# First-layer expert blocks in runs of six, with one product cut in two at each run's head, and another division of the routing among three engines

## The chip, the cores and the metric

The kernel runs on one core of a Trainium2 chip. The time is the device time of one execution in microseconds (us). A core has a matrix engine (TensorE, PE in the rows; its weight loads are listed apart as PEld), three engines for element-wise work (VectorE or DVE, ScalarE or ACT, GpSimd or POOL), and queues of DMA transfers, which SyncE (SP) issues here. Each engine works through its own instructions in order and waits for the others by semaphores.

## What is computed

A decoder layer over 256 tokens of width 1024, in 32-bit floats. The last part takes more than two thirds of the time: a layer of 16384 single-neuron experts, of which every token uses 128 (8 heads, 16 each).

```python
def token_chunk(xc):
    q = (xc @ w_q).reshape(PEER_TOK_CHUNK, PEER_HEADS, 2, half)
    s = jnp.einsum("thpd,hpnd->thpn", q, subkeys)
    s1, i1 = lax.top_k(s[:, :, 0], PEER_TOPK)
    s2, i2 = lax.top_k(s[:, :, 1], PEER_TOPK)
    cand_s = (s1[..., :, None] + s2[..., None, :])
    cand_i = (i1[..., :, None] * PEER_NKEYS + i2[..., None, :])
    top_s, top_pos = lax.top_k(cand_s, PEER_TOPK)
    e = jnp.take_along_axis(cand_i, top_pos, axis=-1)
    g = jax.nn.softmax(top_s, axis=-1)
    a = jax.nn.gelu(jnp.einsum("td,thkd->thk", xc, w_down[e]))
    return jnp.einsum("thk,thkd->td", g * a, w_up[e])
```

Ahead of it stand an attention block, a gating block and a cross-attention, and behind it a normalisation.

## The kernel before

The kernel does not gather experts. It computes all 16384 neurons for all 256 tokens and multiplies by a matrix G that holds the softmax weight of each chosen expert and zero elsewhere.

**First layer.** `down` computes one block of 128 experts: 24 products of 128x128 weights with 256 columns (the tokens), summed in one buffer (tile A, two buffers). Every float is split into a part `hi` that TensorE's format holds and a rest `lw`; for each of the 8 slices of the width come three products, hi weights with `mgh` (hi of the tokens), hi weights with `mgl` (their rest), and lw weights with `mgh`. ScalarE then applies the gelu and frees the buffer (tile aring). There are 128 such blocks, d0 to d127.

**Second layer.** One block takes the gelu of 128 experts times G (tile ga, split into gahl) as stationary operand and adds 12 products of 512 columns to the result (tile y). There are 128 such blocks, called u.

**Weights.** SyncE loads 512 KB for each block (tile raw, four buffers). `conv_to` makes `hi` on ScalarE and then `lw` on the engine that `lo_engine` names, two blocks ahead of use (`LEAD`), three buffers each.

**Order.** `plan` writes the order of d, g and u steps: 27 d blocks; then 16 g steps with 22 d blocks between them (a g step builds a piece of G for the first 64 experts of each group); then 64 u blocks with 42 d blocks spread evenly among them, one at a time; then 16 more g steps with 22 d blocks; then 64 u blocks with the last 15 d blocks spread among them. In the g stretches d blocks stand alone, and six times as a pair, in each of the two.

**Routing.** The first 26 d blocks are the work that TensorE has while the other engines choose the experts. `best` (VectorE) finds the 16 best scores M and places X of each head's halves. XF is X as floats, the first half times 128. `candidates` adds pairs: CS from the scores (VectorE) and CE from the places (GpSimd). Pieces of work on VectorE then choose 16 of the 50 candidates of each head and token (max, match_replace, max_index) and look their places up (L850, L840), until R holds places and weights. A list of estimated lengths decides between which pieces a `down` is written, and with it its `lw`, so VectorE works through the pieces and the `lw` of the d blocks in that order.

Of the kernel before, what the change touches and what calls it, by code (L numbers as in the profile page):

```python
# [21 lines left out]
AF = mybir.ActivationFunctionType  # L22
OP = mybir.AluOpType
# [4 lines left out]
S = 256  # L28
KD = 8
# [3 lines left out]
QI = 64  # L33
# [7 lines left out]
D0, D1 = 22, 4  # L41
# [2 lines left out]
NC = sum(NCAND)  # L44

N_XO, N_PQ = 4, 16
FIRST = 5


def plan():  # L50
    steps = []
    nd = 0

    def d():
        nonlocal nd
        if nd < 128:
            steps.append(("d", nd))
            nd += 1

    def g(q):  # L60

        first, room = nd, RING + q * QI - nd
        for s in range(S // TG):
            steps.append(("g", q, s))
            while nd < first + (s + 1) * room * TG // S:
                d()

    for _ in range(D0 + D1 + 1):
        d()
    g(0)  # L70
    done, want_end = 0, D0 + D1 + 1 + QI - nd
    for n in range(QI):
        steps.append(("u", n))
        want = (n + 1) * want_end // QI
        while done < want:
            d()
            done += 1
    g(1)
    left = 128 - nd
    done = 0  # L80
    for n in range(QI):
        steps.append(("u", QI + n))
        want = min(left, (n + 1) * left // (QI - 8))
        while done < want:
            d()
            done += 1
    return steps


def body(tc, I, out, dbg=None):  # L90
# [3 lines left out]
    V, A, P, T, SY = nc.vector, nc.scalar, nc.gpsimd, nc.tensor, nc.sync  # L94
# [26 lines left out]
    def lo_engine(m):  # L121
        kind, idx = stream[m]
        if kind == "f":
            return V if idx < nf - N_PQ + 4 else P
        if kind == "d" and idx < FIRST:
            return P
        return V

# [34 lines left out]
    def sl(k):  # L163
        return (slice(None), k, slice(None))
# [12 lines left out]
    def mm3(ps, w, wsl, x, xsl, start, stop):  # L177
        (wh, wl), (xh, xl) = w, x
        T.matmul(ps, wh[wsl], xh[xsl], start=start, stop=False)  # L179
        T.matmul(ps, wh[wsl], xl[xsl], start=False, stop=False)  # L180
        T.matmul(ps, wl[wsl], xh[xsl], start=False, stop=stop)  # L181
# [197 lines left out]
    for c in range(4):  # L379
        for nm in ("q", "k"):  # L380
            first = c == 0
            ps = tblock(take("f"), xg, mid=(sqp.matmul if nm == "q" else rope_norm) if first else None)
# [139 lines left out]
    for c in range(4):  # L522
        ps = tblock(take("f"), xg)
# [270 lines left out]
    def mblock():  # L794
        return pp.tile([128, 512], F32, name="m", bufs=2)

    def down(i2):
        w = take("d")
        ps = pp.tile([128, S], F32, name="A", bufs=2)
        for k in range(KD):  # L800
            mm3(ps, w, (slice(None), slice(k * 128, k * 128 + 128)), h3, sl(k), k == 0, k == KD - 1)
        a = gp.tile([128, S], F32, name="aring", bufs=RING)
        A.activation(a, ps, AF.Gelu_apprx_tanh)  # L803
        Aq[i2] = a
# [3 lines left out]


    XF = rp.tile([128, 8, 2, 2, 16], F32, name="XF", bufs=1)  # L810
    V.tensor_copy(XF, X1)
    V.tensor_scalar(XF[:, :, :, 0], XF[:, :, :, 0], 128.0, None, op0=OP.mult)
    CS = rp.tile([128, 8, 2, NC], F32, name="CS", bufs=1)
    CE = rp.tile([128, 8, 2, NC], F32, name="CE", bufs=1)

# [46 lines left out]
    def piece(us, fn, *args):  # L862
        work.append((us, lambda: fn(*args)))

    piece(2.7, candidates, CS, M1, V)
    for (h, t) in ht:
        piece(0.12, V.max, M2[:, h, t, 0:8], CS[:, h, t])
    for (h, t) in ht:
        piece(0.18, V.match_replace, rep2[:, h, t], M2[:, h, t, 0:8], CS[:, h, t], LOW)
# [4 lines left out]
    for (h, t) in ht:  # L874
        piece(0.18, V.max_index, X2[:, h, t, 8:16], M2[:, h, t, 8:16], rep2[:, h, t])
    piece(0.4, V.tensor_copy, XP, X2.rearrange("p h t k -> p (h t) k"))
    piece(0.0, P.tensor_sub, gw, M2, M2[:, :, :, 0:1].to_broadcast([128, 8, 2, 16]))
    for (p, c) in ranks:
        piece(0.15 + 2 * 16 * (17 - p) / 960, lookup, p, c)
    piece(0.3, fold)  # L880
    n, spent = 0, 0.0
    for (us, fn) in work:
        fn()
        spent += us
        while n < D0 and spent > 1.55 * (n + 1) - 2.5:
            down(n)
            n += 1
            if n == FIRST - 2:
                candidates(CE, XF, P)
    while n < D0:  # L890
        down(n)
        n += 1
# [142 lines left out]
    for n, x in enumerate(rest):  # L1035
        if x[0] == "u" and x[1] >= 128 - TAILN:
            break
        if x[0] != "g":
            for nxt in rest[n + 1:n + 3]:
                if nxt[0] == "u" and nxt[1] // QI in Gq:  # L1040
                    up_a(nxt[1])
                    later.append(lambda i2=nxt[1]: up_b(i2))
        if x[0] == "d":
            down(x[1])
            if x[1] == 127:
                A.activation(warm, ones, AF.Sqrt)
        elif x[0] == "g":
            if ng_ < len(gsteps) and gsteps[ng_][1] == x[1]:
                gprep(gsteps[ng_][1], gsteps[ng_][2])
                ng_ += 1  # L1050
            gstep(x[1], x[2])
        else:
            up_a(x[1])
            up_b(x[1])
            w = take("u")
            for t in range(2):
                umm(w, UP[x[1]], t)
            del UP[x[1]]
            if x[1] == QI - 12:
                gprep_a(1, 0)  # L1060
            if x[1] == QI - 9:
                gprep_b(1, 0)
            if x[1] == QI - 6:
                gprep_c(1, 0)
                ng_ += 1
# [118 lines left out]
```

## Time and profile before

| | |
|---|---|
| median of 3 runs | 1043.78 us (1043.71 to 1044.43) |
| the profiled execution, its own time | 1042.34 us |
| its span, first to last instruction | 1040.6 us |
| TensorE busy | 1026.7 us, 99% of the span |
| VectorE, ScalarE, GpSimd busy | 73%, 57%, 6% |
| chain that ended last | 89% TensorE, 8% VectorE |

The profile has the start and duration of every instruction, and what an engine waited for. Products overlap on TensorE, and their listed ends are modelled, so the pace of products is read from the number that starts in a stretch, not from their durations.

### The profile page before, as it was taken

Reading aid. Unit: us, or ns where it says so; the run is one execution under the profiler, and the core shown is the slowest. Engines: PE = TensorE matmul, PEld = TensorE weight load, DVE = VectorE, ACT = ScalarE, POOL = GpSimd, SP = SyncE. Lnnn points to the kernel's source line nnn. Section 1 sums busy time; section 2 is a strip of 40 time slices with the busy share of each in tenths; the row PEclk is TensorE's granted clock in tenths of the full one; section 3 lists DMA queues with packets and bytes.
Section 4 is the critical chain, followed back from the end, with each engine's and each line's share of the span. In section 5 each row is a group of like instructions: output and inputs, shape, how many; then the busy total and the mean of one; then the engine's idle time right before and its main releaser. Section 6 shows DMA issues by size and latency. Waiting matters only on the chain.

```text
span 1040.6 us, 19734 instructions
## 1 busy us (share of the span) xinstructions
PE 1026.7 (99%) x7862; PEld 951.5 (91%) x7862; DVE 760.2 (73%) x1505; ACT 594.4 (57%) x936; POOL 58.1 (6%) x51
## 2 busy tenths in 40 slices
PE   8999999999999899999999999999999999999997
PEld 7989999999999899998889889889999988888886
DVE  6765787789999899865556555565799666666666
ACT  6865745576644477754444544445677645454454
POOL 0400000006730000000000000000000000000000
PEclk9999999999999999999999999999999999999999
DMA  8743655555456434555555565555543555555552
GB/s 283 241 134 130 204 165 176 167 185 162 164 174 202 152 123 149 157 184 191 192 191 193 187 198 185 191 193 184 164 154 130 187 196 188 197 188 198 187 198 103
DMA packets 52076, 185.84 MB, mean 179 GB/s; under 512 B 5904, under 2 KB 6544, under 8 KB 51856
## 3 DMA queue, kind: packets, MB, share of 16 engines
q1 hardware_dynamic: 51264, 183.20, 53.8%
q8 instruction: 61, 1.00, 0.4%
q0 software_dynamic: 288, 1.05, 0.3%
q10 hardware_dynamic: 432, 0.34, 0.1%
q14 instruction: 31, 0.25, 0.1%
HBM read 183.52 MB, written 1.05 MB: 177 GB/s over the span
## 4 chain that ended last, share of the span: by engine, by line
PE 89%; DVE 8%; ACT 1%; DMA 1%; issue 1%; DVEq 0%; ACTq 0%
PE y L1016 11%; PE y L1019 11%; PE y L1015 11%; PE A L179 10%; PE A L181 9%; PE A L180 9%; PE mm L179 6%; PE mm L180 6%; PE mm L181 6%; DVE lw L142 3%; PE m L988 2%; PE m L987 2%; DVE jk L850 1%; DMA raw<-in_wf 1%; DVE acc L840 1%; PE nat L313 1%
## 5 line engine op out<-in xcount | busy, mean ns | idle before, releaser
L142 DVE TENSOR_TENSOR lw<-raw,hi 128x1024 fp32r<-128x1024 f32 (+1 forms) x310 | 378.8, 1223 | 229.4 <-ACT hi L140 228.8
L140 ACT CAST hi<-raw 128x1024 fp32r<-128x1024 f32 (+1 forms) x341 | 355.3, 1043 | 189.4 <-issue 142.9
L181 PE MATMUL A<-mgh,lw 128*128 128x256 f32 x1024 | 287.5, 281 | 3.1 <-DVE lw L142 3.1
L179 PE MATMUL A<-mgh,hi 128*128 128x256 f32 x1024 | 290.1, 283 | 0.0
L180 PE MATMUL A<-mgl,hi 128*128 128x256 f32 x1024 | 287.2, 281 | 0.0
L181 PEld LDWEIGHTS A<-mgh,lw 128*128 128x128 f32 x1024 | 195.9, 191 | 3.5 <-DVE lw L142 3.5
L1015 PE MATMUL y<-hi,gahl 128*128 128x512 f32 x504 | 196.1, 389 | 0.0
L1016 PE MATMUL y<-lw,gahl 128*128 128x512 f32 x504 | 196.1, 389 | 0.0
L180 PEld LDWEIGHTS A<-mgl,hi 128*128 128x128 f32 x1024 | 193.5, 189 | 2.2
L179 PEld LDWEIGHTS A<-mgh,hi 128*128 128x128 f32 x1024 | 193.0, 189 | 2.2
L1019 PE MATMUL y<-hi,gahl 128*128 128x512 f32 x504 | 155.1, 389 | 0.0
L803 ACT ACTIVATE aring<-A 128x256 f32<-128x256 f32 x128 | 49.2, 385 | 162.2 <-PE A L181 162.1
L179 PE MATMUL mm<-xgh,hi 128*128 128x256 f32 x416 | 118.5, 285 | 0.2 <-DVE q L369 0.2
L181 PE MATMUL mm<-xgh,lw 128*128 128x256 f32 x416 | 116.0, 279 | 0.0
L180 PE MATMUL mm<-xgl,hi 128*128 128x256 f32 x416 | 116.0, 279 | 0.0
L1019 PEld LDWEIGHTS y<-hi,gahl 128*128 128x128 f32 x504 | 94.6, 188 | 19.6
L1015 PEld LDWEIGHTS y<-hi,gahl 128*128 128x128 f32 x504 | 94.6, 188 | 17.4
L1016 PEld LDWEIGHTS y<-lw,gahl 128*128 128x128 f32 x504 | 94.6, 188 | 17.4
L179 PEld LDWEIGHTS mm<-xgh,hi 128*128 128x128 f32 x416 | 78.4, 188 | 1.2 <-issue 0.7
L181 PEld LDWEIGHTS mm<-xgh,lw 128*128 128x128 f32 x416 | 78.6, 189 | 0.0
L180 PEld LDWEIGHTS mm<-xgl,hi 128*128 128x128 f32 x416 | 78.4, 188 | 0.1
L989 ACT ACTIVATE G<-m 128x512 f32<-128x512 f32 x64 | 65.9, 1140 | 5.0 <-PE m L988 2.2
(274 smaller groups left out, 1239.9 us busy)
## 6 DMA issues: line engine op xcount, KB each, us to landing
raw<-in_wd SPq DMA_DIRECT2D x128, 512.0 KB, 3.8
raw<-in_wu SPq DMA_DIRECT2D x128, 512.0 KB, 4.1
raw<-in_wf SPq DMA_DIRECT2D x83, 512.0 KB, 4.0
memT<-in_memT SPq DMA_DIRECT2D x1, 1024.0 KB, 6.9
out_y<-raw SPq DMA_DIRECT2D x3, 256.0 KB, 2.0
raw<-in_wf SPq DMA_DIRECT2D x2, 256.0 KB, 4.1
xT<-in_xT SPq DMA_DIRECT2D x2, 256.0 KB, 5.7
xT<-in_xT SPq DMA_DIRECT2D x1, 512.0 KB, 8.2
```

Source lines behind the costliest of these rows:

```text
L140: A.copy(hi[:, ps], raw[:, ps])
L142: lo_engine(m).tensor_sub(lw[:, ps], raw[:, ps], hi[:, ps].bitcast(F32))
L179: T.matmul(ps, wh[wsl], xh[xsl], start=start, stop=False)
L180: T.matmul(ps, wh[wsl], xl[xsl], start=False, stop=False)
L181: T.matmul(ps, wl[wsl], xh[xsl], start=False, stop=stop)
L803: A.activation(a, ps, AF.Gelu_apprx_tanh)
L987: T.matmul(ps[:, t], a1[at], bh[at], start=True, stop=False)
L988: T.matmul(ps[:, t], a1[at], bl[at], start=False, stop=True)
L989: A.activation(Gq[q][:, :, s * TG + c:s * TG + c + 8].rearrange("p i t -> p t i"), ps, AF.Copy, scale=1.0 / 16384.0)
L1015: T.matmul(yps[t][z], gh[:, tsl(t)], wh[:, zs], start=False, stop=False, skip_group_check=True)
L1016: T.matmul(yps[t][z], gh[:, tsl(t)], wl[:, zs], start=False, stop=False, skip_group_check=True)
L1019: T.matmul(yps[t][z], gl[:, tsl(t)], wh[:, zs], start=False, stop=False, skip_group_check=True)
```

## The change

Four things change.

- `plan` rounds the number of d blocks that should have been written down to a multiple of `RUN` = 6 in both u stretches. Where single d blocks stood among the u blocks, seven runs of six stand in the first stretch, and two of six and one of three in the second, with 9 to 23 u blocks between them.
- `down` first runs all 16 products with hi weights, then the 8 with lw weights. With `cut`, the second product is issued as two, of 240 and of 16 columns. `cut` is set for d1, and for every later d block that follows something else and is followed by another d block: 7 + 3 run heads in the u stretches, and the 12 pairs in the g stretches.
- XF is made by ScalarE from X, in two instructions. GpSimd makes the `lw` of d0, d1, d4, d5, d6 and d7 (before: d0 to d4). `begin` adds a small GpSimd subtraction that reads the first max of the candidates, ahead of the `lw` of d4 in GpSimd's queue; the rest of that subtraction (gw) is cut in three.
- The estimates by which `down` is written between the routing pieces are new (`PACE`, `now`).

```diff
@@ plan @@
-        want = (n + 1) * want_end // QI
+        want = (n + 1) * want_end // QI // RUN * RUN if n < QI - 1 else want_end
...
+        want = want if want == left else want // RUN * RUN
@@ lo_engine @@
-        if kind == "d" and idx < FIRST:
+        if kind == "d" and idx in LO_POOL:
             return P
@@ down @@
-    def down(i2):
+    def down(i2, cut=False):
         w = take("d")
         ps = pp.tile([128, S], F32, name="A", bufs=2)
-        for k in range(KD):
-            mm3(ps, w, (slice(None), slice(k * 128, k * 128 + 128)), h3, sl(k), k == 0, k == KD - 1)
+        order = [(k, 0, x, 0, S) for k in range(KD) for x in (0, 1)] + [(k, 1, 0, 0, S) for k in range(KD)]
+        if cut:
+            k, a, x, _, _ = order[1]
+            order[1:2] = [(k, a, x, 0, 240), (k, a, x, 240, S)]
+        for n, (k, a, x, c0, c1) in enumerate(order):
+            T.matmul(ps[:, c0:c1], w[a][:, k * 128:(k + 1) * 128], h3[x][:, k, c0:c1], start=n == 0,
+                     stop=n == len(order) - 1)
@@ XF @@
-    V.tensor_copy(XF, X1)
-    V.tensor_scalar(XF[:, :, :, 0], XF[:, :, :, 0], 128.0, None, op0=OP.mult)
+    for p in range(2):
+        A.activation(XF[:, :, :, p], X1[:, :, :, p], AF.Copy, scale=(128.0, 1.0)[p])
@@ the routing pieces @@
+    def begin():
+        candidates(CS, M1, V)
+        V.max(M2[:, 0, 0, 0:8], CS[:, 0, 0])
+        P.tensor_sub(gw[:, 0, 0, 0:8], M2[:, 0, 0, 0:8], M2[:, 0, 0, 0:1].to_broadcast([128, 8]))
...
-    n, spent = 0, 0.0
+    n, now = 0, 4.0
     for (us, fn) in work:
+        while n < D0 and now >= PACE * n + 2.0:
+            down(n, n == 1)
+            n += 1
+            if n + 1 not in LO_POOL:
+                now += 1.2
+            if n == 6:
+                candidates(CE, XF, P)
         fn()
-        spent += us
-        while n < D0 and spent > 1.55 * (n + 1) - 2.5:
-            down(n)
...
+        now += us
@@ the steps after routing @@
-            down(x[1])
+            down(x[1], rest[n - 1][0] != "d" and rest[n + 1][0] == "d")
```

VectorE at the start of the routing stage, before (the last lines of `best`, then XF, the candidates CS and the first max of the choice; a name's number tells its buffer):

```order
L739 MAX_INDEX X_2876<-M_2875,rep 128x8 x2
L811 CAST XF<-X_2876 128x512
L812 TENSOR_SCALAR XF<-XF 128x16x16
L821 TENSOR_TENSOR CS<-M_2875 128x16x16
L821 TENSOR_TENSOR CS<-M_2875 128x16x8
L821 TENSOR_TENSOR CS<-M_2875 128x16x5
L821 TENSOR_TENSOR CS<-M_2875 128x16x4
L821 TENSOR_TENSOR CS<-M_2875 128x16x3
L821 TENSOR_TENSOR CS<-M_2875 128x16x2 x3
L824 TENSOR_TENSOR CS<-M_2875 128x16x8
L863 MAX M_3759<-CS 128x8 x9
L142 TENSOR_TENSOR lw<-raw,hi 128x1024
```

and now:

```order
L742 MAX_INDEX X_2876<-M_2875,rep 128x8 x2
L145 TENSOR_TENSOR lw<-raw,hi 128x1024 x2
L829 TENSOR_TENSOR CS<-M_2875 128x16x16
L829 TENSOR_TENSOR CS<-M_2875 128x16x8
L829 TENSOR_TENSOR CS<-M_2875 128x16x5
L829 TENSOR_TENSOR CS<-M_2875 128x16x4
L829 TENSOR_TENSOR CS<-M_2875 128x16x3
L829 TENSOR_TENSOR CS<-M_2875 128x16x2 x3
L832 TENSOR_TENSOR CS<-M_2875 128x16x8
L875 MAX M_3759<-CS 128x8
L871 MAX M_3759<-CS 128x8 x15
L871 MATCH_REPLACE rep_3761<-M_3759,CS 128x50 x16
```

XF has left VectorE, the `lw` of d2 and d3 stand ahead of the candidates, and the `lw` that came after nine max instructions comes later.

ScalarE at the same place, before (S is the copy of the last scores that `best` reads, `hi` is that of d2, aring the gelu of d0):

```order
L756 COPY S_2717<-at 128x256 x2
L140 CAST hi<-raw 128x1024
L803 ACT_TABLE_LOAD
L803 ACTIVATE aring<-A 128x256
L140 CAST hi<-raw 128x1024
```

and now:

```order
L759 COPY S_2717<-at 128x256 x2
L820 ACTIVATE XF<-X_2876 128x16x16 x2
L143 CAST hi<-raw 128x1024
L811 ACT_TABLE_LOAD
L811 ACTIVATE aring<-A 128x256
L143 CAST hi<-raw 128x1024
```

The two XF instructions stand between the copies of the scores and the `hi` of d2; the table load and the gelu of d0 come behind both.

TensorE at the head of the first run in the u stretch, before (the end of a u block, then a d block):

```order
L1019 MATMUL y_3750<-hi,gahl 128x512
L1019 MATMUL y_3751<-hi,gahl 128x512
L179 MATMUL A<-mgh,hi 128x256
L180 MATMUL A<-mgl,hi 128x256
L181 MATMUL A<-mgh,lw 128x256
L179 MATMUL A<-mgh,hi 128x256
L180 MATMUL A<-mgl,hi 128x256
L181 MATMUL A<-mgh,lw 128x256
```

and now:

```order
L1037 MATMUL y_3750<-hi,gahl 128x512
L1037 MATMUL y_3751<-hi,gahl 128x512
L808 MATMUL A<-mgh,hi 128x256
L808 MATMUL A<-mgl,hi 128x240
L808 MATMUL A<-mgl,hi 128x16
L808 MATMUL A<-mgh,hi 128x256
L808 MATMUL A<-mgl,hi 128x256
L808 MATMUL A<-mgh,hi 128x256
```

The second product stands in two parts, and the products with lw weights no longer alternate with the others.

## Rows read from the trace of the kernel before

**Rows 1.** The page: the span, and the busy time of each engine.

```profile
span 1040.6 us, 19734 instructions
...
PE 1026.7 (99%) x7862; PEld 951.5 (91%) x7862; DVE 760.2 (73%) x1505; ACT 594.4 (57%) x936; POOL 58.1 (6%) x51
```

**Rows 2.** Busy time of each engine by stage: stretch in us from the start of the span, its length, then for each engine its busy time and (x) its instructions, the granted TensorE clock, the DMA share and GB/s. The last products of the expert stage without routing: first G pass, first half of the second layer, second G pass, second half of the second layer.

```profile
358.46:445.24 86.78, 86.46 (x1104) 85.21 (x1103) 79.05 (x98) 62.78 (x80) 0.00 (x0) 1.00 0.44 137
445.24:737.00 291.76, 291.76 (x1770) 261.87 (x1769) 174.01 (x235) 141.63 (x210) 0.00 (x0) 1.00 0.59 191
737.00:817.50 80.50, 80.49 (x1051) 79.44 (x1050) 73.41 (x87) 61.42 (x78) 0.00 (x0) 1.00 0.45 146
817.50:1012.20 194.70, 194.70 (x1034) 168.55 (x1033) 124.81 (x184) 95.60 (x142) 0.00 (x0) 1.00 0.58 194
```

**Rows 3.** The same view for the products of one tile alone, TensorE only (stretch, length, busy time, count, clock, DMA). Tile A is the result of a first-layer block, 24 products of 256 columns; tile mm is that of the projections in the front part, products of the same shape. The first row is the first block of the routing stage; the next two are the first and the last of five pairs of blocks in the G passes that took 5.54 to 5.56 us, the next two the first and the last of seven pairs that took 5.75; then one block among the second layer's.

```profile
281.76:284.60 2.84, 2.83 (x24) 1.00 0.57 191
374.86:380.40 5.54, 5.53 (x48) 1.00 0.33 104
801.34:806.90 5.56, 5.55 (x48) 1.00 0.35 105
399.76:405.51 5.75, 5.74 (x48) 1.00 0.37 111
811.77:817.52 5.75, 5.74 (x48) 1.00 0.43 124
450.68:453.51 2.83, 2.82 (x24) 1.00 0.54 194
...
146.14:163.25 17.11, 17.11 (x153) 1.00 0.69 217
```

**Rows 4.** Where TensorE goes from the second layer (tile y, 512 columns) to a first-layer block: the timeline (start, duration, engine, line, operation, operands), then the windows of tile y over two second-layer blocks, and of tile nat (products of 512 columns in the front part) right behind the mm stretch of rows 3.

```profile
450.24 0.61 PE L1019 MATMUL y<-hi,gahl 128*128 128x512 f32 x2
450.69 0.28 PE L179 MATMUL A<-mgh,hi 128*128 128x256 f32 x1
450.81 0.28 PE L180 MATMUL A<-mgl,hi 128*128 128x256 f32 x1
...
445.24:450.68 5.44, 5.43 (x24) 1.00 0.69 243
...
163.25:168.75 5.50, 5.49 (x24) 1.00 0.66 197
```

**Rows 5.** The timeline of TensorE where a G step (64 columns) is followed by the first pair of the five.

```profile
374.84 0.19 PE L988 MATMUL m<-bl,a 128*128 128x64 f16 x1
374.87 0.36 PE L179 MATMUL A<-mgh,hi 128*128 128x256 f32 x1
375.07 0.28 PE L180 MATMUL A<-mgl,hi 128*128 128x256 f32 x1
375.19 0.28 PE L181 MATMUL A<-mgh,lw 128*128 128x256 f32 x1
```

**Rows 6.** The timelines of VectorE (DVE) and of GpSimd (POOL) at the start of the routing stage; in brackets the idle time before the row and what ended it.

```profile
286.16 0.29 DVE L739 FIND_INDEX8 X<-M,rep 128x8 uint32<-128x128 f32 x1
286.48 2.48 DVE L811 CAST XF<-X 128x512 f32<-128x512 uint32 x1
289.20 4.93 DVE L821 TENSOR_TENSOR CS<-M 128x256 f32<-128x256 f32 x8
294.49 1.10 DVE L863 MAX8 M<-CS 128x8 f32<-128x50 f32 x9
...
279.55 2.38 POOL L142 TENSOR_TENSOR lw<-raw,hi 128x1024 fp32r<-128x1024 f32 x1 [1.03 <-ACT hi L140]
286.28 2.40 POOL L142 TENSOR_TENSOR lw<-raw,hi 128x1024 fp32r<-128x1024 f32 x1 [0.42 <-ACT hi L140]
289.11 2.44 POOL L142 TENSOR_TENSOR lw<-raw,hi 128x1024 fp32r<-128x1024 f32 x1 [0.43 <-ACT hi L140]
291.51 2.80 POOL L821 TENSOR_TENSOR CE<-XF 128x256 f32<-128x256 f32 x8
```

**Rows 7.** The timeline of ScalarE (ACT) at the same place.

```profile
282.05 0.37 ACT L756 COPY S<-at 128x256 f32<-128x256 f32 x1 [0.41 <-PE at L755]
282.32 1.06 ACT L140 CAST hi<-raw 128x1024 fp32r<-128x1024 f32 x1
283.39 1.28 ACT L803 ACT_TABLE_LOAD   x1
284.88 0.38 ACT L803 ACTIVATE aring<-A 128x256 f32<-128x256 f32 x1 [0.20 <-PE A L181]
```

**Rows 8.** The routing stage: the `lw` on VectorE from the first max of the candidates to R (a group of rows: count, busy us, mean ns, idle before); its next `lw` behind R; then TensorE around its longest wait and at the step behind the stage, then the stretch after the wait in the view of rows 2.

```profile
L142 DVE TENSOR_TENSOR lw<-raw,hi 128x1024 fp32r<-128x1024 f32 x19 | 23.2, 1221 | 0.0
...
350.22 2.35 DVE L142 TENSOR_TENSOR lw<-raw,hi 128x1024 fp32r<-128x1024 f32 x2
...
348.47 0.28 PE L180 MATMUL A<-mgl,hi 128*128 128x256 f32 x1
351.49 0.38 PE L181 MATMUL A<-mgh,lw 128*128 128x256 f32 x1 [2.75 <-DVE lw L142]
...
358.46 0.60 PE L924 MATMUL m<-ident,R 128*128 128x128 f32 x4
...
352.05:355.47 3.42, 3.42 (x18) 3.42 (x17) 1.66 (x2) 0.00 (x0) 0.00 (x0) 0.50 0.86 260
```

More of the change, by code (lines that the diff above doesn't have):

```diff
@@ L46 @@
 N_XO, N_PQ = 4, 16
-FIRST = 5
+PACE = 2.75
+LO_POOL = (0, 1, 4, 5, 6, 7)
+RUN = 6
 def plan():
@@ L863, in piece @@
         work.append((us, lambda: fn(*args)))
-    piece(2.7, candidates, CS, M1, V)
-    for (h, t) in ht:
+    def begin():
+        candidates(CS, M1, V)
+        V.max(M2[:, 0, 0, 0:8], CS[:, 0, 0])
+        P.tensor_sub(gw[:, 0, 0, 0:8], M2[:, 0, 0, 0:8], M2[:, 0, 0, 0:1].to_broadcast([128, 8]))
+    piece(2.9, begin)
+    for (h, t) in ht[1:]:
         piece(0.12, V.max, M2[:, h, t, 0:8], CS[:, h, t])
@@ L876, in body @@
     piece(0.4, V.tensor_copy, XP, X2.rearrange("p h t k -> p (h t) k"))
-    piece(0.0, P.tensor_sub, gw, M2, M2[:, :, :, 0:1].to_broadcast([128, 8, 2, 16]))
+    piece(0.0, P.tensor_sub, gw[:, 0, 0, 8:16], M2[:, 0, 0, 8:16], M2[:, 0, 0, 0:1].to_broadcast([128, 8]))
+    piece(0.0, P.tensor_sub, gw[:, 0, 1], M2[:, 0, 1], M2[:, 0, 1, 0:1].to_broadcast([128, 16]))
+    piece(0.0, P.tensor_sub, gw[:, 1:], M2[:, 1:], M2[:, 1:, :, 0:1].to_broadcast([128, 7, 2, 16]))
     for (p, c) in ranks:
@@ L880, in body @@
     piece(0.3, fold)
-    n, spent = 0, 0.0
+    n, now = 0, 4.0
     for (us, fn) in work:
-        fn()
-        spent += us
-        while n < D0 and spent > 1.55 * (n + 1) - 2.5:
-            down(n)
-            n += 1
-            if n == FIRST - 2:
-                candidates(CE, XF, P)
+        while n < D0 and now >= PACE * n + 2.0:
[5 more added lines that the diff above has]
+                candidates(CE, XF, P)
+        fn()
+        now += us
     while n < D0:
```

## The prediction

> **What bounds the kernel now.** I read the page first. TensorE is busy for 1026.7 of 1040.6 us [rows 1], so time can be won only where its products start closer together or where it waits. The windows by stage say the same: in both u stretches it is busy without a gap, while VectorE has 174 of 292 us and 125 of 195 us of work [rows 2]. So in those 486 us the pace of the products is the time. The windows of single tiles then show what the page cannot: the same product, 256 columns with a full weight load, runs at two paces. In the long mm stretch 153 products start in 17.11 us; without the two that straddle the edges that is one every 113.3 ns. In a d block among the u blocks 24 start in 2.83 us, one every 117.8 ns [rows 3]. Within the G passes both occur, in pairs of blocks of the same form: five pairs took 5.54 to 5.56 us, seven took 5.75 [rows 3]. The clock is at full speed in all these rows (2.4 GHz), no wait is listed, and the pace once found is kept to the end of the run of blocks, so it is set where the run begins. After u blocks I find only the slow pace: the last two y products start from 450.24 on, the first A products at 450.69 and 450.81, the slow spacing at once [rows 4]. A block at the slow pace costs 2.83 - 24 x 0.1133 = 0.106 us more than at the fast one.
>
> The other place is the routing stage, 281.77 to 358.46. VectorE is the bound there: TensorE waits 2.75 us for one `lw` that stands behind the end of routing, and then the granted clock is 0.50 (1.2 GHz) for 3.42 us, in which 18 products start instead of 30 [rows 8]. That is 2.75 plus about 1.5 us.
>
> **The runs of six.** 57 d blocks stand in the u stretches. If a run finds the fast pace behind its first products, they save 57 x 0.106 = 6.0 us, less 10 heads x 4 products x 4.5 ns = 0.2. Only the head of a run can be wrong now, where before each single block was its own head. The price is the cut: the product of 16 columns needs a weight load of its own, and no product with a full load of this type starts after less than 113 ns [rows 3]. I take 0.117 a cut, 1.2 us for ten. The lower end is nothing (240 and 16 columns together stream as long as 256), the upper end is the 0.20 us that a 256-column product needs before the next one starts when it follows the short products of a G step [rows 5]. Sum: -4.6 us, from -5.8 to -3.8 by those ends.
>
> Whether the cut flips the pace no row shows. For it: the pace depends on nothing but how the run is entered, it is never seen to change back within a run, entries that disturb the rhythm end in both paces (5 against 7 pairs), and a product of 16 columns disturbs it, since it streams in a fraction of the time that the next load takes. Against it: the entry behind u blocks is always the same, so ten heads will all go one way.
>
> The Trainium skill's page "TensorE: Matmul & The Clock Gate" (Back-to-back issue gap) gives the gap of an isolated product as columns / 2.4 + 2.5 ns, 109 ns for 256, and has nothing about what ran before. By that rule order cannot matter and the u stretches would only pay for the cuts. What it gives is the first rival below. The trace disagrees with the rule: one form has two paces, and neither is 109 ns.
>
> The longer runs bring no wait: each u or d block takes 2.7 us or more of TensorE, and VectorE has 174/292 of its time filled [rows 2]; hidden under the same cover are the `hi`, the loads (DMA share 0.59) and the gelu. If the cover failed, it would be at u blocks 52 to 58, where G's preparation is added, and cost some tenths.
>
> **The 12 pairs in the G passes.** Twelve cuts cost 1.4 us. If the seven pairs of 5.75 us take the short spacing, 7 x 0.20 = 1.4 comes back; the other five can be thrown out by the same cut, up to 1.0. I take half of that: +0.5, from 0 to +2.4.
>
> **The routing stage.** Removed from VectorE: XF (2.48 us, of which most is a wait, since it ends when GpSimd's `lw` of 286.28 ends) and two or three of the `lw` in its way; the first CS instruction too ends with GpSimd's next `lw` at 291.5 [rows 6]. The candidates end at 294.5 now.
>
> What is added is a wait on ScalarE. Its XF needs the last result of `best`, which VectorE delivers at 286.45 [rows 6], and it stands ahead of `hi` of d2, which runs at 282.32 now [rows 7]. Queued behind it: that `hi`, the table load, the gelu of d0, `hi` of d3. By the rows: 286.5 + 0.7 for XF (two of the 0.37 us copies) + 1.05 + 1.28 + 0.4 = 289.95. TensorE needs the gelu of d0, because A has two buffers, before it can start d2. It is ready for d2 at 281.77 + 2 x 2.83 + 0.12 = 287.5. So it waits 2.4 us where it did not wait before.
>
> VectorE: `lw` of d2 follows its `hi` (288.25) and that of d3 follows `hi` at 290.9, to 292.05; then the candidates, about 1.4 us with GpSimd held back (an estimate: each CS instruction at the pace of the last 0.40 or below), first max done at 293.6, 1.0 earlier than before. From there to R before: 294.6 to 350.2, 55.6 us with 19 `lw` [rows 8]. Now 16 stand there: 55.6 - 3 x 1.15 = 52.1, plus 0.8 where the `lw` of d8 meets GpSimd's for d7. R at 346.5 to 347.2, 3 us earlier.
>
> GpSimd starts `lw` of d4 at 293.8, to 296.2 (2.40 each [rows 6]); d4 starts at 295.5 to 295.8 and needs it only at its 17th product, 1.8 us in. With the order of before it would be the third product and a wait of about half a microsecond; the new order covers it. d5 to d7 follow with 1 us to spare. After d2 I find no `lw` late: that of d24 is there at 348.5 to 349.1, needed at 351.6. So the 2.75 us wait and the slow clock behind it go, and the 2.4 us wait at d2 comes.
>
> From 289.95, d2 to d25 take 24 blocks: at the fast pace to 355.3, at the slow one to 357.9; before they ended at 358.46 [rows 8]. That is -3.2 or -0.6. Before, this stage ran slow for five blocks and fast after its first wait. Now d2 is entered from a wait for a buffer with its weights loaded, nearest to an entry of the G passes, where 7 of 12 were slow. I take -0.6. If 2.4 us of idling is followed by the slow clock as 2.75 was, 1.5 is lost again: the bounds are -3.2 and +0.9. D1's own cut costs 0.1.
>
> **Sum.** -4.6 + 0.5 - 0.6 + 0.1 = -4.6 us. The profiled execution took 1042.34, so 1037.7 on its scale; the median of the runs shown is 1.44 above it, which gives 1039.2.
>
> **The rivals.** First: the cut flips nothing. Then the u stretches pay 1.2, the G pairs 1.4, and routing gives 0.6 to 3.2: +2.1 to -0.5, 1043.3 to 1045.9. For it speaks that no row shows the fast pace behind a y product; against it that a disturbed entry is fast nearly half the time.
>
> Second: the u blocks slow down. In the front part, right behind fast products, 24 products of 512 columns took 5.50 us, 229 ns each, where y takes 226.7 [rows 4]. If y behind products at the short spacing does the same, some 116 u blocks lose 12 x 2.3 ns each, 3.2 us, and the sum is -1.4: 1042.4. Against it: nat has other weights and other places in memory.
>
> Third, on the other side: the cut breaks the rhythm instead of mending it, and each costs 0.20 us as an entry behind short products does [rows 5], with the pace left slow. Then 23 x 0.20 = 4.6 less 0.6: +4.0, 1047.8. It decides when a cut costs over 0.12 and flips nothing.
>
> **How the numbers follow.** My forecast has 0.62, the first rival 0.18, the second 0.12, the third 0.08. Within the forecast the bounds reach from 1035.5 (routing at the fast pace, G pairs at nothing) to 1042; 1036 to 1041.8 is its own range. To leave out no more than 2 in 10 the range runs from 1035.5 to 1046, which takes in the second rival and most of the first. A measurement of this kernel can tell about 0.2%, 2.1 us, from no change. Faster than that: 0.58 from the forecast. Within it: 0.04 of the forecast, the second rival and 0.06 of the first, 0.22. Slower: 0.20.
>
> **What would show it.** Right: 2.72 to 2.75 us for each d block of a run of six but its first; no wait at the end of routing; a wait of 2 to 2.6 us ahead of d2, ended by ScalarE's gelu; CS done within 2 us. Wrong: 2.83 us in the middle of a run; y at 229 ns; a new wait of TensorE for GpSimd's `lw` of d4 to d7; the clock below 1.00 after 290.

## The result, and the profile after

| | before | after |
|---|---|---|
| median | 1043.71 us (1042.52 to 1044.43, 5 runs) | 1037.22 us (1036.80 to 1039.77, 5 runs) |
| the profiled execution | 1042.34 us | 1036.80 us |
| its span | 1040.6 us | 1035.1 us |

The ratio is 0.9947, with a 95% interval of 0.9931 to 0.9964: 0.5% faster. The forecast was 1039.2 us, within 1035.5 to 1046.0.

The page of the kernel after:

```profile
span 1035.1 us, 19784 instructions
...
PE 1021.6 (99%) x7885; PEld 945.7 (91%) x7885; DVE 754.4 (73%) x1502; ACT 594.8 (57%) x938; POOL 62.5 (6%) x55
```

TensorE is still busy for 99% of the span, as in [rows 1]. By stage, between the first products of each (the columns are those of [rows 2]; the first row is the routing stage):

```profile
283.17:356.39 73.22, 71.34 (x628) 71.14 (x627) 66.60 (x300) 39.53 (x59) 15.49 (x18) 1.00 0.58 183
356.39:443.81 87.42, 87.00 (x1110) 85.77 (x1109) 78.99 (x98) 62.55 (x80) 0.00 (x0) 1.00 0.44 141
443.81:733.21 289.40, 289.40 (x1785) 259.34 (x1784) 174.76 (x237) 141.57 (x210) 0.00 (x0) 1.00 0.61 194
733.21:813.10 79.89, 79.86 (x1049) 78.89 (x1048) 72.69 (x87) 61.37 (x78) 0.00 (x0) 1.00 0.44 143
```

Two windows of the kernel before with the same borders, routing and the first u stretch:

```profile
281.77:358.46 76.69, 73.55 (x627) 73.15 (x626) 72.70 (x303) 38.81 (x57) 11.21 (x14) 0.98 0.55 180
445.25:738.05 292.80, 292.80 (x1778) 262.87 (x1777) 175.05 (x236) 141.63 (x210) 0.00 (x0) 1.00 0.59 192
```

Read one against the other, and with the other stages measured alike, the 5.5 us between the two spans are: the part ahead of routing, whose code is the same, +1.4; routing -3.5; first G pass +0.6; first u stretch -3.4; second G pass +0.4; from there to the end -1.1.

**The runs.** The time from the start of one product to that of the next is called the spacing here (the prediction's pace). Windows of tile A: one run of six, its first block, its second block, then two G pairs.

```profile
471.03:487.49 16.46, 16.46 (x145) 16.42 (x144) 1.92 (x5) 1.00 0.59 192
471.03:473.86 2.83, 2.83 (x25) 2.83 (x25) 0.00 (x0) 1.00 0.61 190
474.00:476.72 2.72, 2.72 (x26) 2.72 (x25) 0.38 (x1) 1.00 0.62 196
372.79:378.62 5.83, 5.83 (x49) 5.80 (x49) 0.38 (x1) 1.00 0.36 108
398.27:403.92 5.65, 5.65 (x49) 5.62 (x49) 0.38 (x1) 1.00 0.37 109
```

145 products start in 16.46 us, 113.5 ns each with the cut; a single block took 2.83 us, 117.8 ns a product [rows 3]. The pairs show both spacings still: 5.65 where [rows 3] have 5.54, 5.83 where they have 5.75, a tenth for the cut each time. The head of the run on the timeline:

```profile
470.58 0.62 PE L1037 MATMUL y<-hi,gahl 128*128 128x512 f32 x2
471.03 0.28 PE L808 MATMUL A<-mgh,hi 128*128 128x256 f32 x1
471.15 0.29 PE L808 MATMUL A<-mgl,hi 128*128 128x240 f32 x2
471.29 0.36 PE L808 MATMUL A<-mgh,hi 128*128 128x256 f32 x1
471.49 0.28 PE L808 MATMUL A<-mgl,hi 128*128 128x256 f32 x1
```

The third row holds both parts of the cut product. The product behind them starts at 471.29 and the one behind that 0.20 us later, an interval that [rows 4] do not have.

There is a second way to see the spacing. In a view that lists the least, median and greatest duration of a tile's products, those at 113.3 ns are listed with 276 ns and those at 117.8 with 281. Here the first u stretch of the kernel after:

```profile
L808 PE MATMUL A<-mgh,lw x335: 276/276/277, 473.0 to 733.0; 128*128 128x256 f32 x168
```

**Routing.** ScalarE at the start of the stage, TensorE at d2, and VectorE's candidates:

```profile
285.55 0.42 ACT L820 ACTIVATE XF<-X 128x256 f32<-128x256 uint32 x1 [1.72 <-DVE X L742]
287.88 0.42 ACT L820 ACTIVATE XF<-X 128x256 f32<-128x256 uint32 x1 [1.92 <-DVE X L742]
288.21 1.03 ACT L143 CAST hi<-raw 128x1024 fp32r<-128x1024 f32 x1
289.26 1.28 ACT L811 ACT_TABLE_LOAD   x1
290.55 0.38 ACT L811 ACTIVATE aring<-A 128x256 f32<-128x256 f32 x1
...
290.99 0.39 PE L808 MATMUL A<-mgh,hi 128*128 128x256 f32 x1 [1.88 <-ACT aring L811]
...
293.05 1.33 DVE L829 TENSOR_TENSOR CS<-M 128x256 f32<-128x256 f32 x8
294.30 0.28 DVE L832 TENSOR_TENSOR CS<-M 128x128 f32<-128x128 f32 x1
```

Against [rows 6, 7]: the candidates' first eight additions take 1.33 us and not 4.93, `hi` of d2 comes behind XF, and TensorE waits for the gelu of d0, 1.9 us. It is the stage's only wait of TensorE; that at the end [rows 8] is gone.

### The profile page after: what moved, and what is told of

The parts are those of the page before. It is cut to its first block, busy times and chain, and to the rows that moved or that the text cites. A ratio compares the mean times of both kernels' runs of the same rounds, so it can differ in the third digit from the quotient of the medians.

```text
span 1035.1 us, 19784 instructions
## 1 busy us (share of the span) xinstructions
PE 1021.6 (99%) x7885; PEld 945.7 (91%) x7885; DVE 754.4 (73%) x1502; ACT 594.8 (57%) x938; POOL 62.5 (6%) x55
## 4 chain that ended last, share of the span: by engine, by line
PE 93%; DVE 3%; ACT 2%; DMA 1%; issue 1%; DVEq 0%; ACTq 0%
PE A L808 33%; PE y L1034 11%; PE y L1033 11%; PE y L1037 11%; PE mm L182 6%; PE mm L183 6%; PE mm L184 6%; PE m L1006 1%; PE m L1005 1%; DMA raw<-in_wf 1%; DVE lw L145 1%; ACT hi L143 1%; PE nat L316 1%; PE nat L318 1%; PE nat L317 1%
## 5 line engine op out<-in xcount | busy, mean ns | idle before, releaser
L808 PE MATMUL A<-mgh,hi 128*128 128x256 f32 x1024 | 246.4, 282 | 1.9 <-ACT aring L811 1.9
L808 PE MATMUL A<-mgl,hi 128*128 128x256 f32 (+2 forms) x1047 | 242.1, 275 | 0.0
L808 PE MATMUL A<-mgh,lw 128*128 128x256 f32 x1024 | 138.0, 277 | 0.0
L808 PEld LDWEIGHTS A<-mgh,lw 128*128 128x128 f32 x1024 | 126.6, 188 | 0.0
```

The source lines that it names most:

```text
L808: T.matmul(ps[:, c0:c1], w[a][:, k * 128:(k + 1) * 128], h3[x][:, k, c0:c1], start=n == 0, stop=n == len(order) - 1)
```

## The experiments

Twelve kernels were run. Stages are compared, since the part ahead of routing differs by up to 2.5 us from one execution to another (see the end). "Intervals" are counted from the starts of the products in the traces.

**The runs without the cut.**

```diff
-            down(x[1], rest[n - 1][0] != "d" and rest[n + 1][0] == "d")
+            down(x[1])
```

> The changed kernel, but no first-layer block behind d25 is cut; d1's cut, the runs of six and the new order of products stay. Theory 1 (the cut at the head brings the runs among the second layer to the 113.3 ns spacing): uncut runs of six keep 117.8 ns, 144 x 117.8 = 16.96 us each against 16.46 with the cut; the first stretch of second-layer blocks goes from 289.4 us back to 292.9, the second (to the end) from 222.0 to 223.2, while the twelve pairs in the G passes save what the cut cost them, 1.06: in all 3.6 us longer, about 1040.8 for the median. Theory 2 (six blocks on end, or the new order of products, bring the short spacing by themselves): the runs stay at 113.3 ns and lose only the price of the cut, the first stretch takes 288.4, and the whole 1035.2.

Measured: 1040.51 us, ratio to before 0.9985 (0.9971 to 1.0000). Its first u stretch, and one run of six:

```profile
443.25:736.05 292.80, 292.80 (x1778) 262.83 (x1776) 174.81 (x236) 141.56 (x210) 0.00 (x0) 1.00 0.59 192
...
470.45:487.42 16.97, 16.97 (x144) 16.91 (x143) 1.93 (x5) 1.00 0.57 188
...
L808 PE MATMUL A<-mgh,lw x332: 281/281/281, 442.8 to 733.1; 128*128 128x256 f32 x166
```

292.80 us, to the hundredth what the kernel before takes with single blocks in another order of products. Theory 1 holds: six blocks on end and the new order are worth nothing, the cut is worth 3.4 us here and 1.1 in the second stretch.

**Two kernels for what it is in the cut.** First the old order of products with the cut kept, then the cut in halves.

```diff
-        order = [(k, 0, x, 0, S) for k in range(KD) for x in (0, 1)] + [(k, 1, 0, 0, S) for k in range(KD)]
+        order = [(k, a, x, 0, S) for k in range(KD) for a, x in ((0, 0), (0, 1), (1, 0))]
```

> The changed kernel with the products of a first-layer block in their old order (for each of the 8 slices hi by hi, hi by lo, lw by hi, instead of all products with hi first and then all with lw); cuts, runs of six and routing stay. Theory 1 (the cut by itself sets the spacing): 113.3 ns in the runs, first stretch 289.4 us. Theory 2 (the new order is needed, too): 117.8 ns, 145 intervals a run at 17.1 us, first stretch 293.5 us and the second stretch 216.6.

```diff
-            order[1:2] = [(k, a, x, 0, 240), (k, a, x, 240, S)]
+            order[1:2] = [(k, a, x, 0, 128), (k, a, x, 128, S)]
```

> The changed kernel with the cut product in halves (128 and 128 columns) instead of 240 and 16. Theory 1 (any break of the even row of products sets the short spacing): first stretch 289.4 us, within 0.2. Theory 2 (it takes a product so short that the next weights are not loaded when it ends; in the row of the changed kernel a part of 16 columns is followed by an interval of 203 ns): the runs stay at 117.8 ns and pay for the cut, first stretch 293.2 to 293.6 us.

A run of six in the one and in the other:

```profile
475.10:491.56 16.46, 16.46 (x145) 16.42 (x144) 1.92 (x5) 1.00 0.61 192
```

```profile
471.87:488.33 16.46, 16.46 (x145) 16.42 (x144) 1.92 (x5) 1.00 0.57 192
```

Both as in the changed kernel, and the first u stretch takes 289.40 us in both: theory 1 twice. For the runs neither the order nor the place of the cut in the product matters; it is enough that one product more starts there. The whole took 1041.44 and 1037.46 us; the first lost 4.1 us in routing, of which below.

**Runs of one.**

```diff
-RUN = 6
+RUN = 1
...
-            down(x[1], rest[n - 1][0] != "d" and rest[n + 1][0] == "d")
+            down(x[1], rest[n - 1][0] == "u" or rest[n - 1][0] == "g" and rest[n + 1][0] == "d")
```

> The changed kernel with runs of one: each first-layer block stands alone among the second layer's, as before, and each has the cut. Theory 1 (each cut brings the short spacing and costs 0.14 us with what follows it): a block takes 24 x 113.3 ns + 0.14 = 2.86 us against 2.83 uncut, so the first stretch's 42 blocks take 292.8 + 1.3 = 294.1 us and the second stretch 0.5 more than before: runs are needed to win. Theory 2 (the cut itself is nearly free, 0.03): 2.75 us a block, 289.4 us as with runs of six.

Measured: 1043.04 us; the second u stretch is 1.8 us longer than with runs, and the first takes 294.76 us:

```profile
442.76:737.52 294.76, 294.76 (x1820) 264.18 (x1818) 175.13 (x237) 141.77 (x210) 0.00 (x0) 1.00 0.58 191
```

All 57 blocks show 113 ns behind the cut (2.86 us, 25 products), so a cut after y never missed. It costs more than one block gains: +0.03 us, and 0.015 more at the passage to y. Theory 1. The cut's price is 0.14 us by this and by the run of six (16.46 - 144 x 0.1133).

**The cut and the wait in routing, one without the other.** Without d1's cut:

```diff
-            down(n, n == 1)
+            down(n)
```

> The changed kernel without the cut in d1; the loop's cuts stay. Theory 1 (the 2.16 us gap ahead of d2 sets TensorE to the short spacing, the cut in d1 is not needed): the routing stage stays at 73.2 us, within 0.2, with d0 and d1 (48 intervals) at 117.8 ns and all behind d2 at 113.3. Theory 2 (d1's cut sets the spacing of the stage): its 550 intervals or so behind d1 go to 117.8 ns, 4.5 ns each, and the stage to 75.7 us.

With XF moved on ScalarE behind the gelu of d5, just ahead of GpSimd's CE:

```diff
-    for p in range(2):
-        A.activation(XF[:, :, :, p], X1[:, :, :, p], AF.Copy, scale=(128.0, 1.0)[p])
...
             if n == 6:
+                for p in range(2):
+                    A.activation(XF[:, :, :, p], X1[:, :, :, p], AF.Copy, scale=(128.0, 1.0)[p])
                 candidates(CE, XF, P)
```

> The changed kernel with ScalarE's two conversions of the indices (XF) issued behind d5, just ahead of GpSimd's sums that read them, so that hi of d2, the table load and the gelu of d0 no longer stand behind them; d1's cut stays. The wait ahead of d2 (1.9 us by ScalarE) should go in any case. Theory 1 (d1's cut alone brings the short spacing): the routing stage goes from 73.2 to 71.3 us and the median to about 1035.3. Theory 2 (the wait brought it, and the cut does not): the stage runs at 117.8 ns from d1 on, 600 x 4.5 ns = 2.7 us more, so 74.0 us and a median of 1038.0.

With both edits:

> As the kernel with the late XF, and d1 not cut either: neither wait nor cut is left at the head of the routing stage. Theory 1 (the spacing is set by the way into a stretch: without a wait and without a cut it stays the 117.8 ns it came with): 24 blocks x 24 x 117.8 ns, the stage takes 73.9 to 74.2 us. Theory 2 (VectorE's and GpSimd's new sharing of the port, not the way in, gave the short spacing): 113.3 ns throughout, 71.2 us.

The routing stage of the three, in this order; the second row is the first kernel behind its wait at d2:

```profile
281.06:355.90 74.84, 72.92 (x627) 72.72 (x626) 66.34 (x300) 39.55 (x59) 15.58 (x18) 0.98 0.57 180
288.90:293.20 4.30, 4.30 (x25) 4.30 (x26) 3.37 (x17) 2.08 (x3) 0.40 (x2) 0.64 0.63 198
```

```profile
282.83:353.89 71.06, 71.06 (x629) 71.06 (x628) 66.00 (x300) 39.44 (x59) 15.56 (x18) 1.00 0.57 188
```

```profile
281.10:354.68 73.58, 73.58 (x627) 73.58 (x626) 66.57 (x300) 39.40 (x59) 15.53 (x18) 1.00 0.57 185
```

With neither wait nor cut all 623 intervals behind the first are 117.8 ns (73.58 us). The cut alone brings 113.3 from d1 on (71.06). Without the cut the spacing turns too, behind the wait (552 intervals of the first kernel), but here the granted clock fell behind the wait, to 0.64 over 4.3 us, and 16 products took 213 ns: +1.61, without which its stage would be 73.23. So theory 1 in all three, though the first kernel's time, 74.84, lies nearer to theory 2's number; the spacing tells them apart. Whether the wait turned it or the low clock behind the wait, this trace does not show; in the kernel before, one interval of 0.67 us at the full clock (at 296.1 us) had the same effect. The kernel with the late XF took 1032.76 us, ratio 0.9909 (0.9892 to 0.9926).

**GpSimd not held back.** With the late XF, and the early small subtraction (`begin`) put back with the rest of gw behind the last maxima:

```diff
         V.max(M2[:, 0, 0, 0:8], CS[:, 0, 0])
-        P.tensor_sub(gw[:, 0, 0, 0:8], M2[:, 0, 0, 0:8], M2[:, 0, 0, 0:1].to_broadcast([128, 8]))
...
+    piece(0.0, P.tensor_sub, gw, M2, M2[:, :, :, 0:1].to_broadcast([128, 8, 2, 16]))
```

> The kernel with the late XF, without the small early GpSimd subtraction (gate head) that makes GpSimd wait for VectorE's first maximum; all of it is done in one piece behind the last maxima. GpSimd then starts lw of d4 right behind that of d1 while VectorE works on the candidates. Theory 1 (the two engines get into each other's way: in rows 6 VectorE's casts and additions took 2.5 and 4.9 us beside GpSimd's lw): VectorE's candidate additions take 3 to 5 us and not 1.6, the first maximum comes 2 to 4 us later; the routing stage has 7 us between R and the transposes, so the stage stays at 71.1 or gets up to 1 us longer where a weight's lw comes late. Theory 2 (they do not): first maximum at the same distance from d0, 8.5 us, stage 71.1.

```profile
288.04 5.75 DVE L827 TENSOR_TENSOR CS<-M 128x256 f32<-128x256 f32 x8
...
281.11:352.17 71.06, 71.06 (x629) 71.06 (x628) 69.54 (x300) 39.45 (x59) 13.39 (x15) 1.00 0.59 187
```

The eight additions take 5.75 us beside GpSimd's `lw` and 1.34 without, and the first maximum comes 12.9 us behind d0's start and not 8.5; the stage does not care, 71.06 us. Theory 1 on VectorE; the delay is hidden. With the late XF that part of the change is worth nothing to the time.

**The rule of before for where blocks stand among routing's pieces.** With the late XF, and the old rule in place of `PACE`:

```diff
-        while n < D0 and now >= PACE * n + 2.0:
...
         fn()
-        now += us
+        spent += us
+        while n < D0 and spent > 1.55 * (n + 1) - 2.5:
```

> The kernel with the late XF, with the rule of before for where first-layer blocks stand among routing's pieces (one block for each 1.55 us of pieces by the old count) instead of the new one (2.75 us a block with 1.2 us for an lw); GpSimd's and ScalarE's shares stay as changed. Theory 1 (the new rule removed the wait of rows 8 at the stage's end): a wait of 2 to 3 us for lw comes back and the low clock behind it, the routing stage takes 73.5 to 75 us instead of 71.1. Theory 2 (the work taken off VectorE, lw of d5 to d7 and the casts, removed it): 71.1 us.

Measured: stage 73.84 us, 1037.68 in all. The time is theory 1's, its reason is not seen: at the stage's end one interval of 0.38 us is left of the wait. What is seen is a late `lw` of d2, on TensorE's list of weight loads:

```profile
289.29 0.19 PEld L808 LDWEIGHTS A<-mgl,hi 128*128 128x128 f32 x1
289.47 0.77 PEld L808 LDWEIGHTS A<-mgh,lw 128*128 128x128 f32 x6
```

The load comes 0.07 us late (0.18 behind the last instead of 0.11; VectorE had ended that `lw` at 289.42), the products stretch once from 113 to 175 ns, and from there 526 intervals are 117.8 ns, which is 2.4 us. Neither theory had that.

It hides theory 1's reason, which is there all the same. VectorE's `lw` of d24 and TensorE's first product that needs it, first with the old rule, then in the kernel with the late XF, whose stage began 0.90 us later:

```profile
350.75 2.35 DVE L145 TENSOR_TENSOR lw<-raw,hi 128x1024 fp32r<-128x1024 f32 x2
352.02 0.50 PE L808 MATMUL A<-mgh,lw 128*128 128x256 f32 x2
...
346.85 1.22 DVE L145 TENSOR_TENSOR lw<-raw,hi 128x1024 fp32r<-128x1024 f32 x1
350.25 0.39 PE L808 MATMUL A<-mgh,lw 128*128 128x256 f32 x2
```

From the first product of d0 on, that `lw` starts at 68.8 us with the old rule, right behind R, and at 64.0 with the new. TensorE gets to the product at 67.4 us with the short spacing and at 70.1 here: on the short spacing it would have waited 2.7 us (an estimate from these rows), and the long one lost nothing more. So the new rule was needed to remove the wait; the work taken off VectorE did not do it alone, and whether the rule alone would have, no run shows.

**A cut in the second layer.** One product of 512 columns is cut behind each run:

```diff
+            if cut and z == 0:
+                for c0, c1 in ((0, 496), (496, 512)):
+                    T.matmul(yps[t][z][:, c0:c1], gh[:, tsl(t)], wl[:, c0:c1], start=False, stop=False,
+                             skip_group_check=True)
+                continue
...
-                umm(w, UP[x[1]], t)
+                umm(w, UP[x[1]], t, t == 0 and rest[n - 1][0] != "u")
```

> The changed kernel with a cut (496 and 16 columns) in the second product of the first second-layer block behind each run of first-layer blocks. Theory 1 (512-column products too have a shorter spacing, which a cut brings): the mean of 226.7 ns falls by one step of 6.7 ns to 220 for the 6 to 10 blocks behind each cut, 24 x 6.7 ns = 0.16 us a block, the first stretch 289.4 - 64 x 0.16 + 8 x 0.14 = 280. Theory 2 (226.7 ns is their only spacing): the cuts only cost, 289.4 + 8 x 0.1 to 0.15 = 290.4.

Measured: first u stretch 290.28 us, y still at 226.7 ns. Theory 2; each of the eight cuts there cost 0.11.

**A kernel that beats both, before and after.** The late XF, no cuts in the G pairs, runs of 21 (first stretch) and of 9 and 6, and a cut in the front's second product at the head of three long runs.

```diff
-RUN = 6
+RUN, RUN2 = 21, 9
...
-            down(x[1], rest[n - 1][0] != "d" and rest[n + 1][0] == "d")
+            down(x[1], rest[n - 1][0] == "u" and rest[n + 1][0] == "d")
...
+            if cut and k == 0:
+                T.matmul(ps, w[0][:, c:c + 128], x[0][:, k], start=True, stop=False)
+                T.matmul(ps[:, 0:240], w[0][:, c:c + 128], x[1][:, k, 0:240], start=False, stop=False)
+                T.matmul(ps[:, 240:S], w[0][:, c:c + 128], x[1][:, k, 240:S], start=False, stop=False)
+                T.matmul(ps, w[1][:, c:c + 128], x[0][:, k], start=False, stop=False)
+                continue
```

> The kernel with the late XF, with four further edits: no cut in the twelve pairs of the G passes; the first stretch's 42 first-layer blocks in two runs of 21 and the second's 15 in runs of 9 and 6, each with one cut at its head; and one cut in the front's blocks at the head of three long runs of 256-column products (the third of the gelu branch at 121.6 us, 96 products, at 117.8 ns in all six profiles so far; and the heads of the two runs of 216 at 138 and 169 us, at 113.4 ns in some profiles and 117.8 in others). Theory 1 (a cut at the head brings 113.3 ns for as long as products follow one another, at about 0.14 us a cut): front 0.29 shorter at the first, and at each 216 run 0.14 longer where it had the short spacing and 0.7 to 0.9 shorter where it had the long; first stretch 289.40 - 5 x 0.14 = 288.7; G passes 86.8 and 79.5; in all about 1030.8, with less scatter between executions. Theory 2 (the spacing falls back within a run, so that six blocks are about as long as it holds): the runs of 21 show 117.8 ns behind some block, and the first stretch takes 290 to 291. Theory 3 (21 first-layer blocks on end ask for weights faster than they come, or than ScalarE and VectorE convert them): gaps in the runs of 21, first stretch longer than 289.4.

Measured: 1032.33 us, ratio 0.9912 (0.9897 to 0.9927). One run of 21 (tile A), and the first u stretch:

```profile
527.77:585.03 57.26, 57.26 (x505) 57.22 (x504) 7.68 (x20) 1.00 0.60 193
...
440.73:729.35 288.62, 288.62 (x1781) 258.66 (x1779) 174.62 (x236) 141.68 (x210) 0.00 (x0) 1.00 0.61 194
```

The runs of 21 hold 113.4 ns over all 505 products, first u stretch 288.62: theory 1 there, and nothing of theories 2 and 3. G passes 87.2 and 79.5. In the front the spacing stayed long behind two of the three cuts: 11.49 us for the 97 products at 121 us, and the second run of 216 stayed at 117.8 (25.55). The first run of 216 stood at 113.3, as it also does in six of the twelve traces without a cut there. The next kernel cuts the eighth product there:

```diff
-            if cut and k == 0:
+            if cut and k == 2:
```

> The kernel with the late XF, uncut pairs in the G passes, runs of 21 (first stretch) and of 9 and 6 (second), and the cut at the head of the three long front runs moved from their second product to their eighth. In the kernel where the second product was cut, the 201 to 203 ns interval that follows small products came at the same place, and two of the three runs stayed at 117.8 ns. Theory 1 (a cut sets the short spacing only where the products around it already follow one another evenly): all three runs reach 113.3 ns from the eighth product on, 11.39 becomes 11.1 us at 121 us, and the two runs of 216 take 24.75 and 24.65 us; in all 0.3 us shorter than the best executions and 1.0 than the usual ones of the kernel with the late XF, 1031.0 by the median. Theory 2 (in the front, whose products change weights in another order, no cut sets the spacing): 11.5 us, and the runs of 216 at either spacing plus 0.1; about 1032.3.

Measured: 1030.62 us (1030.08 to 1031.20), ratio 0.9881 (0.9865 to 0.9898). The three front runs, tile mm:

```profile
120.83:131.91 11.08, 11.08 (x97) 11.08 (x97) 1.11 (x3) 0.00 (x0) 1.00 0.58 191
137.48:162.24 24.76, 24.76 (x217) 24.72 (x217) 6.65 (x17) 0.00 (x0) 1.00 0.60 189
167.73:192.36 24.63, 24.63 (x217) 24.58 (x216) 3.39 (x8) 0.00 (x0) 1.00 0.54 173
```

All three stand at 113.3 ns behind the cut. In the first two the spacing turned at the cut; in the third it had turned two intervals ahead of it. The first stood at 117.8 in all twelve traces with an uncut front (11.39 us), so there the cut is what made it short, in one trace. The two runs of 216 stand at 113.3 without any cut in six and in eight of the twelve, so they show little.

Why the early cut missed is not shown. Theory 1's reason, the 0.20 us interval behind small products, fits the first run alone. The other miss, at 168 us, stood behind products of 512 columns, as the heads behind y do, where no cut missed.

## Why the prediction was right, and where not

- **The runs: right.** -4.6 was forecast, -4.5 measured (-3.4 and -1.1). The spacing turned in all ten heads, as "ten heads will all go one way" allowed; that it would turn rested on the G pairs and was a chance taken, not read from a row. The cut's price, taken as 0.117 us, measured 0.14. The gain of a block, 0.106 us, is right, but not by the subtraction that stands there: 2.83 - 24 x 0.1133 is 0.111. From the starts of the products, 24 intervals of 117.75 ns against 24 of 113.3 are 0.106.
- **"Never seen to change back within a run": true of all the runs among the u blocks, not of the front.** In four traces a front run turned to 117.8 ns in its middle (last section).
- **The first rival** (nothing flips) is what the uncut runs show, without the price of the cuts: 292.80 us. The Trainium skill's page "TensorE: Matmul & The Clock Gate" (Back-to-back issue gap), which the prediction set beside it, gives 109 ns for an isolated product of 256 columns, and says that in a stream of loads and products both together set the spacing. The rows here are such a stream, so they do not test the 109 ns, and the prediction took too much from it. They hold 113.3 ns for up to 505 products on end or 117.8 ns for 623, which the page does not have; the measurement decides.
- **The second rival** (y at 229 ns): false, y stays at 226.7 in the first u stretch. **The third** (the cut costs 0.20 and flips nothing): false on both counts behind y; in the front, with the second product cut, it did flip nothing in two of three cases, at 0.1 us.
- **The G pairs: right in sign, mis-sized.** +0.5 was forecast. Between the two profiles it was +1.06. Over ten traces with the cut the passes sum to 167.0 us on the mean, over four without it to 166.4: +0.7. The cut moved more pairs to the shorter spacing (77 of 120, against 17 of 48), but costs a tenth in each.
- **Routing: the mis-sized term.** The steps came as forecast: the wait at the end went, a wait ahead of d2 came (1.9 us against 2.4, since the first XF instruction ran at 285.55, while `best` still worked on the second half), and no `lw` of GpSimd was late. R was ready at 349.4, about a microsecond later than forecast when the 1.4 us of the front are taken off, with no one waiting for it. What failed is "I take -0.6": the spacing behind d2 was taken from the pairs of the G passes, 117.8 ns, and it was 113.3. The bound of -3.2 given with it is about what came (-3.5). Counted from the intervals of the stage, above 113.3 ns each:

| us | long waits of TensorE | products at the low clock | at 117.8 ns | other |
|---|---|---|---|---|
| before | 3.47 | 1.59 | 0.56 | 0.37 |
| after | 2.04 | 0 | 0.12 | 0.25 |

  Waits -1.4, the low clock -1.6, the spacing -0.4. The +0.9 end (low clock behind the new wait) is real too: in five of the seven profiled executions with this wait the clock fell behind it, for 1.4 to 1.6 us. The profiled one of the change was not among them. With the long spacing behind it as well (the old order of products) the stage took 77.29 us, 0.6 more than before.
- **The new wait was the change's own loss.** Without it (late XF) the stage takes 2.2 us less.
- **What was not foreseen:** the 1.4 us in the front, which the diff does not touch. That -5.5 lies near -4.6 is partly luck: routing gave 3.0 more than forecast, while the front took 1.4 and the G pairs 0.6.

## What to carry to other kernels

Where TensorE never waits, look at the spacing of equal products in every long run: if one form has two, a break on purpose (a product issued in two parts) at the head of the run can be tried for 0.14 us; here it pays only over more than one block of 24 products, so let blocks stand in long runs. Look at that spacing again behind every edit: in one trace a weight that came 0.07 us late turned it back for nearly the rest of the stage. When work is moved to another engine, count what stands behind it there: XF cost ScalarE 0.8 us and TensorE 1.9, and issuing it behind d5 took that wait away.

## What the runs showed of the hardware that was not expected

- One form of product (256 columns, full load) runs at 113.3 or 117.8 ns, and each was held for long (505 products; 623 products). It turned at small stalls: to the short one at a product cut in two and at one interval of 0.67 us, to the long one at a load 0.07 us late, and either way across a wait of 1.9 us with the low clock behind it. Why there are two, no run shows.
- It can turn inside a run with no wait and no cut. In four of the twelve traces whose front is the same code, the first of the two front runs of the next point turned to the long one some 60 products in, at a single interval of 0.12 to 0.13 us; in the kernel before it met an interval of 0.13 us at the same product and stayed short. In the kernel after, ahead of that interval (59 intervals) and behind it (154):

```profile
138.66:145.35 6.69, 6.69 (x61) 6.69 (x60) 1.40 (x4) 0.00 (x0) 1.00 0.38 111
145.47:163.61 18.14, 18.14 (x157) 18.14 (x155) 5.12 (x14) 0.00 (x0) 1.00 0.70 218
```

- The same code does not always take the same one. Two front runs of 216 products, at the same clock, in the kernel before (first fence) and after (second):

```profile
138.63:163.26 24.63, 24.63 (x216) 24.59 (x216) 6.67 (x17) 0.00 (x0) 1.00 0.60 190
168.75:193.27 24.52, 24.52 (x216) 24.47 (x215) 3.40 (x8) 0.00 (x0) 1.00 0.55 173
```

```profile
138.44:163.73 25.29, 25.29 (x216) 25.24 (x216) 6.70 (x17) 0.00 (x0) 1.00 0.61 188
169.24:194.69 25.45, 25.45 (x216) 25.39 (x215) 3.39 (x8) 0.00 (x0) 1.00 0.52 165
```

  In the twelve traces with this front the first of these runs is long, in whole or in its greater part, in six, the second in four. That is 1.6 us between two executions, and where the 1.4 us of the front come from. It is half of the scatter of the times after (1036.8 to 1039.8); the low clock behind the wait at d2 would be another 1.6, but a time without its trace cannot be assigned.
- In the kernel with the old order of products, routing came out of the low clock behind the wait at 117.8 ns (556 intervals on end, 2.5 us), in the four others with the low clock there at 113.3. Whether the order or chance did it stays open.
- GpSimd's `lw` holds up VectorE's additions of two operands in memory: 5.75 us against 1.34 for the same eight. The Trainium skill's page "SBUF — State Buffer" (SBUF: two separate sides) says that the two share a port pair, which the one that starts holds for its whole instruction. The trace of the kernel without the early GpSimd subtraction agrees: the third and the seventh of the eight took 2.43 and 2.39 us, from 288.58 and 291.29 on, each as long as the `lw` beside it. Its GpSimd, and the shortest, median and longest of the eight in ns:

```profile
288.48 2.43 POOL L145 TENSOR_TENSOR lw<-raw,hi 128x1024 fp32r<-128x1024 f32 x1 [7.21 <-ACT hi L143]
291.20 2.43 POOL L145 TENSOR_TENSOR lw<-raw,hi 128x1024 fp32r<-128x1024 f32 x1 [0.29 <-ACT hi L143]
...
L827 DVE TENSOR_TENSOR CS<-M x8: 182/252/2434, 288.0 to 293.6; 128x32 f32<-128x32 f32 x3, 128x256 f32<-128x256 f32 x1, 128x128 f32<-128x128 f32 x1, 128x80 f32<-128x80 f32 x1
```
